# Softmax reciprocals for two heads at once, and inverse norms by logarithm and exponential, in a hybrid decoder layer

## The chip, the cores and the metric

The kernel runs on one core of one Trainium2 chip. The metric is device time of one launch in microseconds (us); lower is better. Before the change the median of three runs is 1438.42 us (1437.84 to 1440.45).

The core's engines are named as the profile names them: PE is TensorE (matmuls; PEld is its weight load), DVE is VectorE, ACT is ScalarE, POOL is GpSimd, SP issues the transfers. Each engine takes its instructions in the order in which they were built; an instruction waits until what it needs from the other engines is done, and what is queued behind it on the same engine waits too.

## What is computed

One decoder layer over 1024 tokens of width 1024, in fp32. Two places of it are touched by the change (R stands for the four heads of a group):

```python
def rms_norm(x, g):
    y = x * lax.rsqrt(jnp.mean(x * x, axis=-1, keepdims=True) + RMS_EPS)
    return y * g

# attention of one block of 128 queries: three branches, each with its own softmax and gate
p_sel = masked_softmax(ss, causal)            # selected blocks: with 16 of 16 blocks, all keys up to the query
p_win = masked_softmax(sw, window of 512)     # sliding window
o = g[..., 0:1] * o_cmp + g[..., 1:2] * o_sel + g[..., 2:3] * o_win

x = x + mix @ w_out                           # mix: NSA heads and HGRN heads side by side
h = rms_norm(x, norm_ffn)                     # the FFN's input
gate, up = split(h @ w_gate_up)
x = x + (silu(gate) * up) @ w_down
```

## The kernel before

The layer runs in stages on the one core: input projection and HGRN heads, keys and values, attention together with the output projection, gate and up products (Winograd's form), and the down product. The change lies in the attention stage and in its end, where the first products of the feed-forward part begin.

**Attention.** Queries go in blocks of 128 tokens (`qb` 0 to 7). A unit is a block, a group of four heads (`g`) and a branch (`b`: 0 selected, 1 window); there are 32 units. The loop over units first issues `score` of a unit and then `values` of the unit before it. The framework's scheduler then orders the instructions of each engine by itself, so that both mix; nothing in the source fixes that order.

- `score` (lines 892 to 928) goes over four heads. PE makes the scores in PSUM (lines 915 to 918), DVE takes the negated row maximum `nm` (line 923), ACT the exponential into `pbig` with the row sum in `den` (line 924), DVE the reciprocal of `den` (line 925), and POOL multiplies the weights by reciprocal and gate (line 926). For `qb` of 4 and more the scores take one of two double banks, `ps_s`, which comes free when the exponential has read it.
- `values` (lines 930 to 943) goes over blocks of keys. PE transposes the weights of four heads into `ps_t` (line 937, two banks), ACT copies them into the high part of `ph` (line 939), DVE makes the low part (line 940), and PE multiplies both with the values (lines 941 and 942).

**Output projection and norm.** When a block of queries is finished, two output tiles (`nsa_out`, lines 807 to 824) follow in the gaps: twelve matmuls each (lines 114 to 116), added to the residual `x1` on DVE (line 590). After the second one `norm_stats` (lines 251 to 256) squares the token tile on ACT with the row sum in `n_ss` (line 254) and calls `rsqrt` (lines 118 to 127). That is twelve instructions on one column, all on DVE: three to start (lines 121 to 123) and three rounds of three (lines 125 to 127). Seven tiles are then scaled by ACT (line 821) and by the gain on POOL (line 822); the last, tile 7, is done by one DVE instruction (line 819).

**Into the feed-forward part.** `operand` (lines 796 to 804) transposes half tiles on PE and splits them on ACT (line 803) and DVE (line 804). Tile 7's norm falls into this stretch, so that its small DVE instructions stand between such splits.

The few lines that matter most:

```python
V.reciprocal(den, den)
G.tensor_scalar(pp, pp, den, gates[:, qb, h * 3 + 1 + b:h * 3 + 2 + b], op0=OP.mult, op1=OP.mult)
...
for _ in range(3):
    V.tensor_tensor(t, y, y, op=OP.mult)
    V.scalar_tensor_tensor(t, t, -0.5, v, op0=OP.mult, op1=OP.mult)
    V.scalar_tensor_tensor(y, t, 1.5, y, op0=OP.add, op1=OP.mult)
```

## Time and profile before

| | us |
|---|---|
| median of three runs | 1438.42 (1437.84 to 1440.45) |
| span of the profiled execution, first to last instruction | 1436.3 |
| runs' median less that span | 2.1 |
| PE busy | 1371.1 (95%) |
| DVE busy | 1110.9 (77%) |
| ACT busy | 622.9 (43%) |
| POOL busy | 506.4 (35%) |

The profile is of one execution; it gives its span, and its time outside the span isn't given apart, so the difference of 2.1 us between the runs' median and the span stands for what lies around it. Attention lies between about 415 and 765 us of the span, and the gate and up products follow. PE's granted clock is 0.987 of full speed over the span and 0.99 to 1.00 in the stretches that matter here. A busy PE isn't PE at its peak, since ends of matmuls are modelled.

### The profile page before, as it was taken

What the parts mean: (1) busy time and instruction counts of PE and PEld (TensorE: products, weight loads), DVE (VectorE), ACT (ScalarE), POOL (GpSimd) and SP (SyncE); (2) the same over time, 40 slices, a digit from 0 to 9 for tenths busy, and PEclk for the clock granted to TensorE, in tenths of its full rate; (3) what the DMA queues carried; (4) which work ended last, traced back from release to release, by engine and by line L of the source; (5) the groups of instructions that cost most, each with busy time, mean ns of one, the idle gap of its engine ahead of it and who ended that gap; (6) DMA issues with size and microseconds to landing.
All of it is one profiled execution on the core that took longest, in us unless ns stands there. A gap on an engine that the chain in (4) does not pass through costs nothing.

```text
span 1436.3 us, 20189 instructions
## 1 busy us (share of the span) xinstructions
PE 1371.1 (95%) x7224; PEld 1134.7 (79%) x7224; DVE 1110.9 (77%) x1948; ACT 622.9 (43%) x1211; POOL 506.4 (35%) x412
## 2 busy tenths in 40 slices
PE   8699999999999999999998999999999999987998
PEld 6578888999977777787776888888888888865887
DVE  8985889725787888889877877777777765899796
ACT  5652333323346666566655333333333323423442
POOL 7610111102034442443427423332233310379573
PEclk9899999999999999999999999999999999988999
DMA  8541110120130001000003322222222228742252
GB/s 278 192 117 45 30 30 16 41 72 27 45 133 1 1 1 59 30 16 30 16 30 89 103 88 89 80 73 82 89 75 88 88 89 313 275 151 96 81 161 95
DMA packets 103923, 122.63 MB, mean 85 GB/s; under 512 B 5872, under 2 KB 65424, under 8 KB 103824
## 3 DMA queue, kind: packets, MB, share of 16 engines
q1 hardware_dynamic: 103824, 121.35, 26.1%
q8 instruction: 57, 0.93, 0.3%
q14 instruction: 42, 0.34, 0.1%
HBM read 101.41 MB, written 19.92 MB: 84 GB/s over the span
## 4 chain that ended last, share of the span: by engine, by line
PE 74%; DVE 17%; issue 3%; ACT 2%; POOL 2%; DMA 1%; SPq 0%; ACTq 0%; POOLq 0%; DVEq 0%
PE bank L115 8%; PE bank L116 7%; PE a L114 7%; PE bank L114 7%; PE a L115 7%; PE a L116 7%; DVE wop L108 4%; PE ps_t L114 4%; PE ps_t L115 4%; PE ps_t L116 4%; PE ps_t L937 3%; PE a L941 2%; PE a L942 2%; PE ps_t L469 1%; PE ps_s L915 1%
## 5 line engine op out<-in xcount | busy, mean ns | idle before, releaser
L107 ACT ACTIVATE wop<-rpage 128x512 fp32r<-128x512 f32 x180 | 112.2, 627 | 172.2 <-PE bank L116 70.8
L926 POOL TENSOR_SCALAR pbig<-pbig,den,gates 128x640 f32<-128x640 f32 (+7 forms) x128 | 103.7, 815 | 165.3 <-DVE den L925 146.3
L108 DVE TENSOR_TENSOR wop<-rpage,wop 128x512 fp32r<-128x512 f32 x180 | 146.6, 818 | 16.9 <-ACT wop L107 14.9
L940 DVE TENSOR_TENSOR ph<-ps_t,ph 128x512 fp32r<-128x512 f32 x126 | 84.3, 683 | 17.8 <-ACT ph L939 17.0
L939 ACT ACTIVATE ph<-ps_t 128x512 fp32r<-128x512 f32 x126 | 72.7, 595 | 48.9 <-PE ps_t L937 40.0
L1088 POOL TENSOR_TENSOR tmp<-tmp,rpage 128x512 f32<-128x512 f32 x21 | 35.2, 1676 | 131.4 <-DVE wop L108 131.4
L937 PE MATMUL ps_t<-ident,pbig 128*128 128x128 f32 x504 | 78.2, 274 | 2.1 <-POOL pbig L926 2.1
L115 PE MATMUL bank<-wop 128*128 128x512 f32 x175 | 70.8, 405 | 9.4 <-DVE wop L108 9.4
L475 POOL TENSOR_TENSOR kp<-kp,fp 128x256 f32<-128x256 f32 x28 | 20.3, 725 | 162.2 <-PE bank L452 110.7
L108 DVE TENSOR_TENSOR wop<-tmp,wop 128x512 fp32r<-128x512 f32 x42 | 40.1, 956 | 38.7 <-ACT wop L107 37.7
L937 PEld LDWEIGHTS ps_t<-ident,pbig 128*128 128x128 f32 x504 | 60.7, 140 | 11.5 <-POOL pbig L926 3.2
L1048 POOL TENSOR_TENSOR tmp<-rpage 128x512 f32<-128x512 f32 x20 | 26.3, 1315 | 123.0 <-DMA rpage<-in_w_gate_up_dram 123.0
L114 PE MATMUL bank<-wop 128*128 128x512 f32 x175 | 69.5, 398 | 0.0
L116 PE MATMUL bank<-wop 128*128 128x512 f32 x175 | 69.4, 398 | 0.0
L114 PE MATMUL a<-whi,hT_h 128*128 128x256 f32 (+1 forms) x232 | 66.6, 287 | 0.0
L115 PE MATMUL a<-wlo,hT_h 128*128 128x256 f32 (+1 forms) x232 | 66.4, 286 | 0.0
L116 PE MATMUL a<-whi,hT_l 128*128 128x256 f32 (+1 forms) x232 | 66.2, 285 | 0.0
L924 ACT ACTIVATE pbig<-ps_s,nm 128x640 f32<-128x640 f32 (+3 forms) x64 | 55.9, 876 | 23.5 <-DVE nm L923 17.5
L923 DVE TENSOR_REDUCE nm<-ps_s 128x1 f32<-128x640 f32 (+3 forms) x64 | 58.1, 914 | 4.1 <-PE ps_s L918 2.7
L941 PE MATMUL a<-ph,kv 128*128 128x512 f32 x132 | 58.6, 444 | 1.7 <-ACT ph L939 1.0
L107 ACT ACTIVATE wop<-tmp 128x512 fp32r<-128x512 f32 x42 | 26.6, 633 | 76.8 <-POOL tmp L1088 44.1
L942 PE MATMUL a<-ph,kv 128*128 128x512 f32 x132 | 57.0, 432 | 2.8 <-DVE ph L940 2.3
(514 smaller groups left out, 4541.5 us busy)
## 6 DMA issues: line engine op xcount, KB each, us to landing
rpage<-in_w_gate_up_dram SPq DMA_DIRECT2D x86, 256.0 KB, 3.3
rpage<-in_w_down_dram SPq DMA_DIRECT2D x40, 512.0 KB, 4.3
act_d<-th SPq DMA_DIRECT2D x44, 256.0 KB, 2.1
rpage<-in_w_in_dram SPq DMA_DIRECT2D x14, 512.0 KB, 5.0
xn<-in_x_dram SPq DMA_DIRECT2D x8, 512.0 KB, 3.9
wraw<-in_w_in_dram SPq DMA_DIRECT2D x16, 256.0 KB, 3.4
wraw<-in_w_in_dram SPq DMA_DIRECT2D x8, 512.0 KB, 3.6
wraw<-in_w_out_dram SPq DMA_DIRECT2D x8, 512.0 KB, 3.2
```

What stands on the lines that cost most here:

```text
L107: A.activation(hi, src, AF.Copy)
L108: V.tensor_tensor(lo, src, hi.bitcast(F32), op=OP.subtract)
L114: PE.matmul(o, ah, bh, start=first, stop=False)
L115: PE.matmul(o, ah, bl, start=False, stop=False)
L116: PE.matmul(o, al, bh, start=False, stop=last)
L923: V.tensor_reduce(nm, sv, axis=AX.XY, op=OP.max, negate=True)
L926: G.tensor_scalar(pp, pp, den, gates[:, qb, h * 3 + 1 + b:h * 3 + 2 + b], op0=OP.mult, op1=OP.mult)
L937: PE.transpose(pt[:, r * P:(r + 1) * P], wts[r][:, c0:c0 + P], ident)
L939: A.activation(ph[:, 0], pt, AF.Copy)
L940: V.tensor_tensor(ph[:, 1], pt, ph[:, 0].bitcast(F32), op=OP.subtract)
L941: PE.matmul(o, vst[b][:, kb, g, :], ph[:, 0], start=b == 0 and kb == kb0, stop=False)
L942: PE.matmul(o, vst[b][:, kb, g, :], ph[:, 1], start=False, stop=False)
```

## The change

`score` keeps the row sums of two heads in the two columns of one tile, takes one reciprocal after every second head, and only then lets POOL scale both heads' weights. `norm_stats` no longer calls `rsqrt`: DVE makes mean square plus epsilon `v`, ACT takes its logarithm and the exponential of minus half of that, and DVE refines the result by one Newton step of three instructions. `rsqrt` stays for the other norms. Comments and docstrings were dropped too, which alters no instruction.

```diff
@@ norm_stats
         ss = small.tile([P, 1], F32, name="n_ss", tag="n_ss")
         rs = small.tile([P, 1], F32, name="n_rs", tag="n_rs", bufs=NT)
+        v = small.tile([P, 1], F32, name="n_v", tag="n_v")
+        t = small.tile([P, 1], F32, name="n_t", tag="n_t")
         A.activation(junk, src, AF.Square, accum_out=ss)
-        rsqrt(rs, ss, 1, 1.0 / D, EPS)
+        V.tensor_scalar(v, ss, 1.0 / D, EPS, op0=OP.mult, op1=OP.add)
+        A.activation(t, v, AF.Ln)
+        A.activation(rs, t, AF.Exp, scale=-0.5)
+        V.scalar_tensor_tensor(t, rs, rs, v, op0=OP.mult, op1=OP.mult)
+        V.tensor_scalar(t, t, -0.5, 1.5, op0=OP.mult, op1=OP.add)
+        V.tensor_scalar(rs, rs, t, None, op0=OP.mult)
         return rs
@@ score
             res = []
+            den = None
             for r in range(4):
...
-                den = small.tile([P, 1], F32, name="den", tag="den", bufs=4)
+                if r % 2 == 0:
+                    den = small.tile([P, 2], F32, name="den", tag="den", bufs=4)
...
-                A.activation(pp.rearrange("p (i n) -> p i n", i=sv.shape[1]), sv, AF.Exp, bias=nm, accum_out=den)
-                V.reciprocal(den, den)
-                G.tensor_scalar(pp, pp, den, gates[:, qb, h * 3 + 1 + b:h * 3 + 2 + b], op0=OP.mult, op1=OP.mult)
+                A.activation(pp.rearrange("p (i n) -> p i n", i=sv.shape[1]), sv, AF.Exp, bias=nm, accum_out=den[:, r % 2:r % 2 + 1])
                 res.append(pp)
+                if r % 2:
+                    V.reciprocal(den, den)
+                    for k in range(2):
+                        gk = (h - 1 + k) * 3 + 1 + b
+                        G.tensor_scalar(res[r - 1 + k], res[r - 1 + k], den[:, k:k + 1], gates[:, qb, gk:gk + 1],
+                                        op0=OP.mult, op1=OP.mult)
             return kb0, res
```

The scheduler orders the engines anew. SP's order is the same row for row. Lines of the changed kernel are 8 to 14 higher than the same lines before.

The first place is ACT, around the norm of token tile 0 (attention of block 5). `rpage,n_ss<-x` is the square with its row sum, `pbig,den` an exponential of scores, `ph` a part of the transposed weights, `x<-x,n_rs` the scaling. Before:

```order
L254 ACTIVATE rpage,n_ss<-x_3665 128x1024
L939 ACTIVATE ph<-ps_t 128x512
L924 ACTIVATE pbig,den<-ps_s,nm 128x768
L939 ACTIVATE ph<-ps_t 128x512
L924 ACTIVATE pbig,den<-ps_s,nm 128x768
L939 ACTIVATE ph<-ps_t 128x512
L924 ACTIVATE pbig,den<-ps_s,nm 128x768
L939 ACTIVATE ph<-ps_t 128x512
L924 ACTIVATE pbig,den<-ps_s,nm 128x768
L939 ACTIVATE ph<-ps_t 128x512 x2
L821 ACTIVATE x_3665<-x_3665,n_rs 128x1024
```

Now:

```order
L257 ACTIVATE rpage,n_ss<-x_3665 128x1024
L953 ACTIVATE ph<-ps_t 128x512
L934 ACTIVATE pbig,den<-ps_s,nm 128x768
L259 ACT_TABLE_LOAD
L259 ACTIVATE n_t<-n_v 128x1
L934 ACT_TABLE_LOAD
L934 ACTIVATE pbig,den<-ps_s,nm 128x768
L260 ACTIVATE n_rs<-n_t 128x1
L934 ACTIVATE pbig,den<-ps_s,nm 128x768
L829 ACTIVATE x_3665<-x_3665,n_rs 128x1024
L953 ACTIVATE ph<-ps_t 128x512
L934 ACTIVATE pbig,den<-ps_s,nm 128x768
```

Beside the logarithm and the exponential stand two table loads, one ahead of each; all eight norms have such a pair, so there are 16 loads more than before (where the program has one, at its start). The `ph` copies, which stood between the exponentials, now come after them.

The second place is PE in the same unit. `a<-ph,kv` are matmuls of `values`, `ps_t<-ident,pbig` transposes, `ps_s` scores, `a<-whi,rpage` and `a<-wlo,rpage` an output tile. Before:

```order
L918 MATMUL ps_s<-cmask,identb 128x128
L941 MATMUL a_5999<-ph,kv_3025 128x512
L937 MATMUL ps_t<-ident,pbig 128x128 x4
L942 MATMUL a_5999<-ph,kv_3025 128x512
L915 MATMUL ps_s<-kv_3025,q 128x384
L916 MATMUL ps_s<-kv_3025,q 128x384
```

Now:

```order
L927 MATMUL ps_s<-cmask,identb 128x128
L951 MATMUL ps_t<-ident,pbig 128x128 x4
L114 MATMUL a_6113<-whi,rpage 128x512
L115 MATMUL a_6113<-wlo,rpage 128x512
L116 MATMUL a_6113<-whi,rpage 128x512
L114 MATMUL a_6113<-whi,rpage 128x512
L115 MATMUL a_6113<-wlo,rpage 128x512
L924 MATMUL ps_s<-kv_3025,q 128x384
L925 MATMUL ps_s<-kv_3025,q 128x384
```

Matmuls of an output tile moved to where two that need `ph` stood, and those that need `ph` moved behind.

The third place is DVE at the last norm, tile 7, among the operand splits. Before:

```order
L127 SCALAR_TENSOR_TENSOR n_rs<-rs_t,n_rs 128x1
L804 TENSOR_TENSOR opB<-bank,opB 128x4x128
L125 TENSOR_TENSOR rs_t<-n_rs 128x1
L804 TENSOR_TENSOR opA<-bank,opA 128x4x128
L126 SCALAR_TENSOR_TENSOR rs_t<-rs_t,rs_v 128x1
L804 TENSOR_TENSOR opC<-bank,opC 128x4x128
L127 SCALAR_TENSOR_TENSOR n_rs<-rs_t,n_rs 128x1
L108 TENSOR_TENSOR wop<-rpage,wop 128x512
L819 SCALAR_TENSOR_TENSOR x_3665<-x_3665,n_rs,rpage 128x1024
L108 TENSOR_TENSOR wop<-epage,wop 128x512
```

Now:

```order
L258 TENSOR_SCALAR n_v<-n_ss 128x1
L812 TENSOR_TENSOR opA<-bank,opA 128x4x128
L812 TENSOR_TENSOR opB<-bank,opB 128x4x128
L261 SCALAR_TENSOR_TENSOR n_t<-n_rs,n_v 128x1
L812 TENSOR_TENSOR opB<-bank,opB 128x4x128
L262 TENSOR_SCALAR n_t<-n_t 128x1
L812 TENSOR_TENSOR opB<-bank,opB 128x4x128
L263 TENSOR_SCALAR n_rs<-n_rs,n_t 128x1
L812 TENSOR_TENSOR opB<-bank,opB 128x4x128
L827 SCALAR_TENSOR_TENSOR x_3665<-x_3665,n_rs,rpage 128x1024
L812 TENSOR_TENSOR opB<-bank,opB 128x4x128 x2
L108 TENSOR_TENSOR wop<-rpage,wop 128x512
```

The scaling of tile 7 (line 819, now 827) stands two `opB` splits, an `opA` and an `opC` split earlier than it did, and the small instructions before it are fewer.

## Rows read from the trace of the kernel before

**Rows 1.** The page's chain that ended last, by engine.

```profile
PE 74%; DVE 17%; issue 3%; ACT 2%; POOL 2%; DMA 1%; SPq 0%; ACTq 0%; POOLq 0%; DVEq 0%
```

**Rows 2.** Busy time by stretch (us): the attention's two parts and its end.

```profile
core 0: us, PE busy (x) PEld busy (x) DVE busy (x) ACT busy (x) POOL busy (x), PEclk, DMA share, GB/s
415.00:560.00 145.00, 141.39 (x865) 112.23 (x864) 116.47 (x288) 93.00 (x246) 61.75 (x84) 0.99 0.03 8
560.00:765.00 205.00, 197.08 (x1110) 153.59 (x1109) 165.43 (x355) 128.10 (x248) 84.72 (x71) 1.00 0.08 30
```

**Rows 3.** Busy time in seven stretches, each from a norm's square to its scaling.

```profile
596.02:609.13 13.11, 12.25 (x69) 9.09 (x68) 12.12 (x28) 9.42 (x17) 5.19 (x5) 1.00 0.17 61
...
sum 83.06, PE 78.16 PEld 59.70 DVE 75.00 ACT 56.84 POOL 26.45; mean PE 11.17 PEld 8.53 DVE 10.71 ACT 8.12 POOL 3.78
```

**Rows 4.** Busy time in the six stretches between those, from 609.13 to 750.20 us.

```profile
sum 77.47, PE 77.03 PEld 60.75 DVE 56.66 ACT 46.22 POOL 36.60; mean PE 12.84 PEld 10.12 DVE 9.44 ACT 7.70 POOL 6.10
```

**Rows 5.** DVE in time order, first norm: start, us, what.

```profile
595.90 1.62 DVE L603 CAST rpage<-qtok 128x512 fp32r<-128x512 f32 x1
597.56 0.69 DVE L604 TENSOR_TENSOR rpage<-qtok,rpage 128x512 fp32r<-128x512 f32 x1
...
606.43 0.84 DVE L126 SCALAR_TENSOR_TENSOR rs_t<-rs_t,rs_v 128x1 f32<-128x1 f32 x1
607.20 0.68 DVE L940 TENSOR_TENSOR ph<-ps_t,ph 128x512 fp32r<-128x512 f32 x1
```

**Rows 6.** PE in time order, first norm: the waits behind those two.

```profile
599.77 0.49 PE L942 MATMUL a<-ph,kv 128*128 128x512 f32 x1 [0.39 <-DVE rs_v L121]
...
607.93 0.50 PE L942 MATMUL a<-ph,kv 128*128 128x512 f32 x1 [0.41 <-DVE ph L940]
```

**Rows 7.** DVE groups by line, 415 to 800 us: busy, mean ns, idle before.

```profile
L925 DVE RECIPROCAL den<-den 128x1 f32<-128x1 f32 x128 | 19.6, 156 | 8.1 <-ACT pbig L924 7.0
L125 DVE TENSOR_TENSOR rs_t<-n_rs 128x1 f32<-128x1 f32 x24 | 7.0, 291 | 0.2
L127 DVE SCALAR_TENSOR_TENSOR n_rs<-rs_t,n_rs 128x1 f32<-128x1 f32 x24 | 6.8, 284 | 0.2
L126 DVE SCALAR_TENSOR_TENSOR rs_t<-rs_t,rs_v 128x1 f32<-128x1 f32 x24 | 6.5, 271 | 0.3
L884 DVE RECIPROCAL c_den<-c_den 128x8 f32<-128x8 f32 x8 | 1.5, 192 | 0.0
L122 DVE TENSOR_SCALAR rs_t<-rs_v 128x1 int32<-128x1 int32 x8 | 1.2, 147 | 0.1
```

**Rows 8.** ACT in time order, the program's start: its one table load.

```profile
0.73 1.28 ACT L433 ACT_TABLE_LOAD   x1 [0.73 <-PEq L1308]
3.00 0.21 ACT L433 ACTIVATE gains<-gains 128x8 f32<-128x8 f32 x1 [0.99 <-DVE gains L432]
```

**Rows 9.** DVE in time order, the program's start.

```profile
2.82 0.16 DVE L432 TENSOR_TENSOR gains<-par_t,gains 128x4 f32<-128x4 f32 x1
```

**Rows 10.** Busy time (us) around the last norm, columns as in Rows 2.

```profile
763.13:779.24 16.11, 10.92 (x66) 7.66 (x64) 15.32 (x27) 10.03 (x18) 12.55 (x9) 1.00 0.52 135
```

**Rows 11.** DVE in time order at the last norm.

```profile
770.05 0.85 DVE L127 SCALAR_TENSOR_TENSOR n_rs<-rs_t,n_rs 128x1 f32<-128x1 f32 x1
...
771.42 0.70 DVE L125 TENSOR_TENSOR rs_t<-n_rs 128x1 f32<-128x1 f32 x1
...
772.65 0.83 DVE L126 SCALAR_TENSOR_TENSOR rs_t<-rs_t,rs_v 128x1 f32<-128x1 f32 x1
...
774.00 0.72 DVE L127 SCALAR_TENSOR_TENSOR n_rs<-rs_t,n_rs 128x1 f32<-128x1 f32 x1
```

**Rows 12.** Waits of PE and its weight load, 415 to 560 us: total, times, longest.

```profile
PE ps_t L937 <- POOL pbig L926: 2.1, 3, 1.4
...
PEld ps_t L937 <- POOL pbig L926: 3.2, 6, 1.7
```

**Rows 13.** POOL's scaling by line: times ns min/median/max over all sizes.

```profile
L926 POOL TENSOR_SCALAR pbig<-pbig,den,gates x128: 443/872/1693, 416.1 to 734.9; 128x640 f32<-128x640 f32 x40, 128x128 f32<-128x128 f32 x16, 128x256 f32<-128x256 f32 x16, 128x384 f32<-128x384 f32 x16
```

## The prediction, made before the changed kernel was run

> **What bounds the kernel now.** I read the page's chain of waits first, then busy time by stretch, then single engines in time order. In the chain PE has 74% and DVE 17%, ACT and POOL 2% each [rows 1]: a saving on DVE can count, a few us on ACT so far cost nothing. The change lies between 415 and about 780 us. In its two long parts PE is busy 141.4 of 145 and 197.1 of 205 us [rows 2], so 3.6 and 7.9 us of idle PE are all that faster other engines could give back there by this view.
>
> Where that idle time lies is the main reading. I cut the second part at the norms of the first seven token tiles, each stretch from its square to its scaling. In those seven stretches, 83.06 us together, PE is busy 78.2 and DVE 75.0, that is 90% of the time, while ACT has 56.8 (68%) [rows 3]. In the six stretches between them PE is busy 77.03 of 77.47 us [rows 4]. So PE loses its time at the norms, where DVE is nearly full, and almost none elsewhere. The first norm shows how: a cast took 1.62 us where its sister instruction took 0.69, and one of the small norm instructions 0.84 us where such a one takes 0.15 without waiting [rows 5, 7]; soon behind each of them PE stands still for 0.39 and 0.41 us [rows 6].
>
> **What leaves DVE.** Of the twelve instructions of a norm, three take 0.15 us and nine 0.27 to 0.29 on average [rows 7]: 3 x 1.2 + 7.0 + 6.8 + 6.5 = 23.9 us for eight norms, 3.0 us each. The new norm has four: three of one input, at 0.15, and one with two tensors, at 0.27, together 0.72 us; that is 2.3 us less per norm, 18 us in all. Of the 128 reciprocals at 0.156 us [rows 7] 64 go, 10 us; two columns instead of one I cost at nothing, because eight take 0.192. In the seven norm stretches DVE then has 75.0 - 16 = 59 us of 83, even before the reciprocals are counted.
>
> **What comes to ACT.** Per norm: a table load, the logarithm, a second load, the exponential. The one load of the trace took 1.28 us and an exponential of eight columns 0.21 [rows 8], so 2 x 1.28 + 2 x 0.21 = 3.0 us in which ACT serves nobody, 24 us for eight norms. In the seven stretches ACT goes from 56.8 to 56.8 + 21 = 77.8 of 83 us, or 94%. DVE and ACT change places: what was the fullest engine beside PE gets air, and the other becomes a little fuller than DVE was, in lumps.
>
> The load's price has an upper bound as well. In the only row, 0.99 us pass from its end at 2.01 to the next activation at 3.00 [rows 8]. The DVE instruction which that activation waited for ended at 2.82 + 0.16 = 2.98 [rows 9], which explains the gap, so I take 1.28; the bounds are 1.28 and 1.28 + 0.99 = 2.27.
>
> The Trainium skill, page "ScalarE: Activation LUTs", section "What ACT_TABLE_LOAD costs", speaks against this change: a switch to another table set is a load of about 1283 ns plus a drain of about 1380 ns, 2.66 us together. The trace agrees on the load [rows 8] and shows no drain, as no switch under way was recorded; by the page's figure, and as an estimate, the sum below would be 16 x 1.38 = 22 us longer, 1466 us.
>
> **Seven norms under attention.** What does a stop of 3.0 us on ACT cost PE? Behind the loads stand the next exponential, which frees a bank for the scores of a later head, and the `ph` copies that the matmuls of `values` need. The pairing adds to this: the reciprocal of a pair on DVE waits for the second head's exponential, which at the first norm is behind both loads, and the Newton step and the next row maximum are queued behind it. The scheduler put five matmuls of an output tile in front of the score, so part is covered. The nearest rows for the rest are the two waits above: 0.93 us lost on DVE became 0.39 of PE, and 0.69 us became 0.41 [rows 5, 6], so about half. Half of 3.0 is 1.5 us per norm. Against it, PE now loses 4.9 / 7 = 0.7 us per norm to a full DVE [rows 3], most of which should return: 0.5. Net +1.0 per norm, **+7 us** for seven. Bounds: -4.9 if the loads are wholly covered and all idle time returns, +21 if all 3.0 us show and nothing returns; with 0.99 us more per load, another 14.
>
> **The last norm.** From 763 to 779 us DVE is busy 15.3 of 16.1 and PE only 10.9 [rows 10]; here DVE is the bound. Four of the small instructions took 0.85, 0.70, 0.83 and 0.72 us [rows 11], 3.1 together, and in the new order none stands there any more. ACT gets 3.0 us, on 10.0 of 16.1 us busy, but its `opB` copies wait behind the loads, and the DVE splits need them. I take half of the gain, **-1.5 us**; bounds -3.1 and +3.0.
>
> **Pairs of heads in the narrow blocks.** POOL scales both heads after the second exponential, so the weights are complete one POOL instruction later. Up to 560 us PE and its weight load wait for POOL in 9 places, 5.3 us [rows 12]; with the shortest scaling, 0.44 us [rows 13], 9 x 0.44 = 4 us is the upper bound, and the 3.6 us of idle PE in this part [rows 2] are the lower one, if fewer reciprocals on DVE let everything run sooner. I take **+0.5 us**. Beyond 560 us I count nothing, since the scaling is covered by a unit of other heads' scores and values; were that cover gone, 16 units x 0.87 us [rows 13] would be 14 us.
>
> **Sum.** +7 - 1.5 + 0.5 = +6 us on the profiled execution: 1436.3 becomes 1442.3 us of span. The median of the runs lies 2.1 us above that span, so I forecast **1444.4 us** (+0.4%).
>
> **Rivals.**
> 1. *DVE's relief wins.* If the moved output matmuls cover the loads, the norm stretches lose their 4.9 us of idle PE and the last norm its 3.1: 1438.4 - 8.0 = 1430.4 us; half of it gives 1434.4. For it: PE waits for DVE at the norms, not for ACT [rows 3, 6]. Against it: ACT at 94% has less air than DVE had, and its new work comes in stops of 3.0 us instead of small pieces between others. It decides if PE has 3 us of work per norm that needs neither `ph` nor a freed score bank; the order shows five matmuls and four transposes.
> 2. *They cancel.* ACT's fullness replaces DVE's and PE loses as much as before: 1438.4 us. For it: 94% against 90%.
> 3. *A load costs more than its row.* With the 0.99 us on each of 16 loads: 1444.4 + 16 = 1460 us. Against it: that gap has its own explanation [rows 8, 9]. For it: the load here ran on an empty engine, and those to come stand between other activations.
>
> The change could fail to do what it says only if loads were merged or scheduled away; the built order shows all 16.
>
> **Chances.** About 0.2% (2.9 us) is what a measurement of this kernel can tell from no change. My forecast, slower by 3 to 12 us, has 0.42; the dearer load, slower by more, 0.16; cancelling 0.22; the relief 0.20. So faster 0.20, same 0.22, slower 0.58. The range is 1434 to 1458 us: it leaves out the better half of rival 1 and the worse part of rival 3, under 2 in 10 together. The forecast's own range is 1441.5 to 1450.
>
> **What would show it.** In the profile of the changed kernel: 17 table loads in all, and the time from a load's end to the next activation on ACT; in the stretches around the seven norms, PE's waits named for ACT (`ph`, exponentials) where DVE stood, and ACT near 78 of 83 us; DVE down by about 28 us in the stage; PE as full as before between the norms; the scaling of tile 7 earlier. I am wrong if PE's idle time at the norms shrinks, if loads are followed by a gap near 1 us, or if PE begins to wait for POOL beyond 560 us.

## The result, and the profile after

The changed kernel takes 1461.17 us (median of 4 runs, 1460.47 to 1461.86) against 1438.69 us of the kernel before on the same chip: the ratio is 1.0156, with an interval of 1.0142 to 1.0171, **22.5 us slower**. The forecast of 1444.4 us had the sign and a good quarter of the size, and the range ended 3 us too early.

The page of the changed kernel: span, busy time and the chain that ended last.

```profile
span 1459.3 us, 20095 instructions
PE 1382.6 (95%) x7224; PEld 1142.8 (78%) x7224; DVE 1094.9 (75%) x1820; ACT 644.4 (44%) x1243; POOL 504.9 (35%) x412
PE 76%; DVE 14%; ACT 5%; issue 3%; POOL 2%; DMA 1%; SPq 0%; POOLq 0%; ACTq 0%; DVEq 0%
```

In the chain ACT has gone from 2% to 5% and DVE from 17% to 14% [rows 1]: both shares have moved the way that the prediction gave. What it did not say stands in the PE row. Before, the 7224 matmuls were busy for 1371.1 us of 1436.3; now the same 7224 matmuls are busy for 1382.6 us of 1459.3. So of the 23.0 us that the span grew, 11.5 are idle time of PE (65.2 before, 76.7 now), and the other 11.5 are matmuls that **took longer**.

The seven stretches from a norm's square to its scaling, now 64.77 us together (start and end in us, then columns as in rows 2); the first and the sixth stretch and the sum.

```profile
597.07:607.12 10.05, 8.44 (x47) 6.02 (x45) 7.15 (x12) 8.43 (x15) 2.89 (x3) 1.00 0.23 80
...
732.85:743.01 10.16, 7.60 (x42) 6.36 (x41) 6.54 (x16) 8.15 (x16) 1.20 (x2) 0.87 0.07 28
...
sum 64.77, PE 49.51 PEld 36.48 DVE 43.77 ACT 58.02 POOL 10.66; mean PE 7.07 PEld 5.21 DVE 6.25 ACT 8.29 POOL 1.52
```

PE is idle for 15.3 us in them, where it was for 4.9 [rows 3]. ACT is busy for 90% of the time and DVE for 68%; before, DVE had the 90% and ACT the 68% [rows 3]. There the two have changed places.

The sixth norm shows the mechanism. First ACT in time order (start, us, what):

```profile
735.68 1.28 ACT L259 ACT_TABLE_LOAD   x1
736.97 0.20 ACT L259 ACTIVATE n_t<-n_v 128x1 f32<-128x1 f32 x1
737.19 1.28 ACT L934 ACT_TABLE_LOAD   x1
738.49 0.79 ACT L934 ACTIVATE pbig<-ps_s,nm 128x640 f32<-128x640 f32 x1
739.18 0.19 ACT L934 ACTIVATION_READ_ACCUMULATOR pbig<-ps_s,nm 128x1 f32 x1
739.27 0.19 ACT L260 ACTIVATE n_rs<-n_t 128x1 f32<-128x1 f32 x1
```

Each load takes 1.28 us, and what follows it starts 0.01 to 0.02 us behind its end. From 735.68 to 738.49, 2.8 us, ACT does nothing for anybody else. Then PE in time order, at the same place:

```profile
736.48 0.39 PE L114 MATMUL a<-whi,rpage 128*128 128x512 f32 x1
739.43 0.38 PE L924 MATMUL ps_s<-kv,q 128*128 128x256 f32 x1 [2.56 <-ACT pbig L934]
739.65 0.39 PE L956 MATMUL a<-ph,kv 128*128 128x512 f32 x1
739.88 0.40 PE L969 MATMUL a<-ph,vc_st 128*128 128x256 f32 x2
740.11 0.40 PE L969 MATMUL a<-ph,vc_up 128*128 128x256 f32 x2
740.35 0.99 PE L808 MATMUL ps_t<-ident,x 128*128 128x128 f32 x4
...
742.23 1.05 PE L951 MATMUL ps_t<-ident,pbig 128*128 128x128 f32 x4
...
744.36 0.60 PE L951 MATMUL ps_t<-ident,pbig 128*128 128x128 f32 x4
```

The next scores need the PSUM bank that the exponential behind the second load frees, so PE stands still for 2.56 us, until that exponential has run. And then four transposes take 1.05 us at 742.23, where four others of the same line take 0.60 us two us later. The windows show what differs; the third number from the end of a row is the granted clock:

```profile
730.00:735.00 5.00, 4.99 (x34) 4.07 (x32) 3.58 (x9) 3.55 (x9) 2.37 (x2) 1.00 0.26 107
735.00:740.00 5.00, 2.44 (x13) 1.64 (x12) 2.08 (x5) 4.40 (x8) 0.00 (x0) 1.00 0.00 0
740.00:745.00 5.00, 5.00 (x26) 4.51 (x25) 3.85 (x9) 4.38 (x9) 1.91 (x1) 0.66 0.00 0
745.00:750.00 5.00, 5.00 (x31) 3.91 (x30) 2.28 (x4) 1.42 (x4) 5.00 (x6) 1.00 0.01 3
```

PE is busy for 2.44 of 5 us in one window, and in the next its granted clock is 0.66 on average; cut finer, it was 0.50 (1.2 GHz of 2.4) from 741 to 743. PE then is busy all the time, for a part of it at half speed. **This stop of ACT is paid twice**: once while PE waits, and again when it has work. Added up over slices of 1 us from 560 to 900 us, one minus the granted clock comes to 13.7 us in the changed kernel and to 0.0 in the kernel before, whose clock does not fall once in this stretch. I call this sum the *lost clock* below. Not all of the 13.7 us stands behind loads. A fall of the clock follows the loads of four of the eight norms (those at 630, 735, 760 and 782 us), 8.5 us together; at the other four it stays at 1.00. One fall, 1.7 us at 576 us, comes before the first load (601.27 us), and one, 3.4 us at 805 us, behind a wait of PE that has no load in it (see the last norm below).

Waits of PE from 560 to 785 us (total, times, longest), the three longest:

```profile
PE ps_s L924 <- ACT pbig L934: 11.2, 9, 2.6
PE a L955 <- ACT ph L953: 5.3, 6, 2.5
PE a L956 <- DVE ph L954: 1.0, 3, 0.5
```

The first two are waits for ACT, for the two things that the prediction had named, exponentials and `ph` copies. The kernel before had waits for ACT there too; its three longest, from 560 to 765 us:

```profile
PE ps_s L915 <- ACT pbig L924: 3.6, 6, 0.9
PE a L942 <- DVE ph L940: 2.3, 6, 0.6
PE a L941 <- ACT ph L939: 0.7, 1, 0.7
```

Beyond 560 us PE waits nowhere for POOL's scaling of the weights (line 940). In the narrow blocks it waits for POOL for 1.5 us and its weight load for 3.2, against 2.1 and 3.2 [rows 12].

On DVE, from the groups by line, what is left of the reciprocals and of the new norm (busy, mean ns, idle before):

```profile
L937 DVE RECIPROCAL den<-den 128x2 f32<-128x2 f32 x64 | 10.2, 159 | 17.2 <-ACT pbig L934 11.6 <-ACT n_rs L260 4.8
...
L261 DVE SCALAR_TENSOR_TENSOR n_t<-n_rs,n_v 128x1 f32<-128x1 f32 x8 | 1.7, 218 | 12.3 <-ACT n_rs L260 12.3
```

The reciprocal of two columns takes 159 ns where one column took 156 [rows 7], so the prediction's nothing for the second column holds. What is new is in the idle column: DVE stands for 12.3 us in front of the Newton step of six norms, waiting for the exponential, with the next row maximum queued behind it.

### The profile page after: what moved, and what is told of

The parts are those of the page before. It is cut to its first block, busy times and chain, and to the rows that moved or that the text cites. A ratio compares the mean times of both kernels' runs of the same rounds, so it can differ in the third digit from the quotient of the medians.

```text
span 1459.3 us, 20095 instructions
## 1 busy us (share of the span) xinstructions
PE 1382.6 (95%) x7224; PEld 1142.8 (78%) x7224; DVE 1094.9 (75%) x1820; ACT 644.4 (44%) x1243; POOL 504.9 (35%) x412
## 4 chain that ended last, share of the span: by engine, by line
PE 76%; DVE 14%; ACT 5%; issue 3%; POOL 2%; DMA 1%; SPq 0%; POOLq 0%; ACTq 0%; DVEq 0%
PE bank L115 8%; PE a L114 8%; PE bank L116 8%; PE bank L114 8%; PE a L115 8%; PE a L116 8%; PE ps_t L114 4%; PE ps_t L115 4%; PE ps_t L116 4%; DVE wop L108 4%; PE ps_t L951 3%; PE a L955 2%; PE a L956 2%; PE ps_t L477 1%; PE ps_s L924 1%
## 5 line engine op out<-in xcount | busy, mean ns | idle before, releaser
L940 POOL TENSOR_SCALAR pbig<-pbig,den,gates 128x640 f32<-128x640 f32 (+7 forms) x128 | 100.3, 794 | 157.9 <-DVE den L937 116.9
L954 DVE TENSOR_TENSOR ph<-ps_t,ph 128x512 fp32r<-128x512 f32 x126 | 84.2, 684 | 20.5 <-ACT ph L953 19.6
L955 PE MATMUL a<-ph,kv 128*128 128x512 f32 x132 | 60.3, 457 | 5.9 <-ACT ph L953 5.3
L956 PE MATMUL a<-ph,kv 128*128 128x512 f32 x132 | 59.2, 448 | 1.5 <-DVE ph L954 1.0
```

The lines of the kernel that those rows point to most:

```text
L940: G.tensor_scalar(res[r - 1 + k], res[r - 1 + k], den[:, k:k + 1], gates[:, qb, gk:gk + 1], op0=OP.mult, op1=OP.mult)
L954: V.tensor_tensor(ph[:, 1], pt, ph[:, 0].bitcast(F32), op=OP.subtract)
L955: PE.matmul(o, vst[b][:, kb, g, :], ph[:, 0], start=b == 0 and kb == kb0, stop=False)
L956: PE.matmul(o, vst[b][:, kb, g, :], ph[:, 1], start=False, stop=False)
```

## The experiments

Every kernel is compared with the kernel before on the same chip; the difference is that of the two medians. Loads counts the table loads of the program; PE busy and idle are the page's, for one profiled execution; lost clock is the sum from 560 to 900 us.

| kernel | loads | median us | against before | PE busy | PE idle | lost clock |
|---|---|---|---|---|---|---|
| before | 1 | 1438.7 | | 1371.1 | 65.2 | 0.0 |
| changed | 17 | 1461.2 | +22.5 | 1382.6 | 76.7 | 13.7 |
| pairs alone | 1 | 1444.5 | +5.3 | 1377.0 | 65.0 | 3.4 |
| new norm alone | 17 | 1460.4 | +21.2 | 1381.3 | 76.2 | 11.9 |
| changed, no switch | 1 | 1443.0 | +3.9 | 1372.2 | 66.9 | 3.4 |
| before and 16 unread loads | 17 | 1457.4 | +18.2 | 1379.1 | 75.0 | 6.8 |
| the same, 14 loads | 15 | 1456.3 | +17.7 | 1382.4 | 73.5 | 10.2 |
| the same, 32 loads | 33 | 1478.9 | +40.0 | 1386.8 | 89.7 | 20.5 |
| new norm, no switch | 1 | 1440.7 | +2.1 | 1373.0 | 65.6 | 5.1 |
| pairs, narrow blocks | 1 | 1440.4 | +1.8 | 1371.8 | 65.5 | 1.7 |
| pairs, wide blocks | 1 | 1443.4 | +4.8 | 1373.0 | 67.0 | 1.7 |
| norms in groups, new | 7 | 1460.4 | +21.6 | 1379.8 | 75.9 | 13.7 |
| norms in groups, old | 1 | 1453.8 | +15.0 | 1378.5 | 72.4 | 13.7 |
| lighter norm on DVE | 1 | 1434.8 | -4.1 | 1370.6 | 62.0 | 0.0 |
| lighter, two rounds | 1 | 1439.2 | -0.2 | 1371.9 | 65.5 | 1.7 |
| lighter and pairs | 1 | 1435.9 | -3.5 | 1372.5 | 60.6 | 1.7 |
| before, one unread DVE op | 1 | 1442.4 | +3.8 | 1374.0 | 65.4 | 0.0 |
| lighter, one unread DVE op | 1 | 1439.2 | +0.6 | 1376.3 | 63.7 | 5.1 |
| 16 unread loads, one DVE op | 17 | 1457.2 | +18.6 | 1381.1 | 74.2 | 8.5 |
| changed, one table set | 3 | 1442.9 | +4.1 | 1377.7 | 64.3 | 6.8 |

**First question: is it the loads, the pairs, or the chain through ACT?** The theory was that the table loads stop ACT and PE pays with idle time and clock. The rivals were the pairs, which hold DVE behind the second head's exponential, and the longer chain DVE, ACT, ACT, DVE. Four kernels tell them apart.

*The pairs alone*: the changed kernel with the old norm.

```diff
         A.activation(junk, src, AF.Square, accum_out=ss)
-        V.tensor_scalar(v, ss, 1.0 / D, EPS, op0=OP.mult, op1=OP.add)
-        A.activation(t, v, AF.Ln)
...
+        rsqrt(rs, ss, 1, 1.0 / D, EPS)
         return rs
```

> The reciprocals of pairs alone, with the old norm: one table load. Theory (the 16 table loads stop ACT, PE idles behind them and its granted clock falls): nothing of the loss is here; 1435 to 1441 us, the granted clock 1.00 at the norms as in the kernel before. Rival (the pairing: a pair's reciprocal and two scalings come later, and everything on DVE and POOL behind them): most of the 22.5 us is here, 1448 us or more, with PE waiting for POOL or DVE beyond 560 us.

Measured: 1444.49 us, ratio 1.0037 (1.0023 to 1.0051), no wait of PE for POOL's scaling beyond 560 us. The bulk of the loss is not here. The time lies between the two windows, 3 us above the theory's and 4 below the rival's, and PE's idle time did not grow at all: its busy time did.

*The new norm alone*: the kernel before with the change's eight new lines in `norm_stats` and one reciprocal per head.

> The new norm alone, with one reciprocal per head: 17 table loads. Theory (loads): 1455 to 1463 us, nearly all of the loss, with the granted clock falling to about 0.5 at several places between 560 and 850 us. Rival (the pairing does it, by holding DVE behind the second head's exponential and so behind the loads): without the pairing under half of the loss, 1438 to 1449 us.

Measured: 1460.36 us, ratio 1.0148 (1.0132 to 1.0164). As the theory has it, nearly the whole loss is there without a pair.

*The changed kernel without a switch of tables.*

```diff
-        A.activation(t, v, AF.Ln)
+        A.activation(t, v, AF.Exp, scale=1e-3)
```

> The changed kernel with the logarithm replaced by an exponential of the same input (scale 0.001), so that ACT's table stays: the same chain ACT, DVE, ACT, ACT, DVE, the same number of instructions, one table load instead of 17. The FFN's inverse norms are other numbers, so what is computed differs. Theory (loads): 1430 to 1440 us, no fall of the granted clock at the norms, PE's idle time in the seven norm stretches back to 5 us or less from 15.3. Rival (the longer chain across three engines, or the new order of instructions, does it without any load): 1452 us or more.

Measured: 1443.04 us, ratio 1.0025 (1.0014 to 1.0035), 18.6 us less than the changed kernel (both against the kernel before on their chip); 3 us above the theory's window and far from the rival's. The chain across the engines costs little.

*Loads that nobody needs*, in the kernel before.

```diff
+        u = small.tile([P, 1], F32, name="n_u", tag="n_u")
+        A.activation(u, ss, AF.Ln)
+        A.activation(u, u, AF.Exp, scale=-0.5)
         rsqrt(rs, ss, 1, 1.0 / D, EPS)
```

> The kernel before, with a logarithm and an exponential of the sum of squares behind each square, whose result nobody reads; the old norm stays on DVE. 17 table loads, and nothing waits for them but what stands behind them on ACT. Theory (a stopped ACT is enough): 1455 to 1466 us, the norms' DVE work not relieved on top. Rival (the loss comes from the norm's results arriving later, by the chain through ACT): 1437 to 1445 us.

Measured: 1457.36 us, ratio 1.0125 (1.0110 to 1.0141). No result waits for these loads; what stands behind them on ACT's queue does. 16 loads cost 18.2 us, or 1.1 us each, 2.3 per norm; the two short activations per norm that bring them are in this price.

**Second question: how does the loss grow, and where?**

*Loads at the first seven norms only* (the two lines under `if tt < NT - 1`, with the tile's number passed in).

> The kernel before with the unread logarithm and exponential behind the squares of token tiles 0 to 6 but not behind that of tile 7: 15 table loads. All eight cost 18.2 us. If each norm's two loads cost the same: about 7/8 of that, 1454 to 1456 us. If the last norm, where DVE is the bound and the copies for DVE's splits wait behind the loads, is dearer than the others, as the granted clock falls there too: 1446 to 1452 us.

Measured: 1456.34 us, 17.7 us above the kernel before, ratio 1.0121 (1.0105 to 1.0136). So the last norm's two loads cost about half a us, with an uncertainty of some 3 us by the two intervals: it is not the dear one, and the other seven cost 2.5 us each.

*Twice the loads.*

```diff
         A.activation(u, ss, AF.Ln)
         A.activation(u, u, AF.Exp, scale=-0.5)
+        A.activation(u, ss, AF.Ln)
+        A.activation(u, u, AF.Exp, scale=-0.5)
```

> The kernel before with twice the unread pairs behind each square: logarithm, exponential, logarithm, exponential; 33 table loads, each norm stops ACT for about 6 us instead of 3. The 16 loads took 18.2 us. If the loss grows with the time that ACT is stopped: 1475 to 1482 us, and more if the second half is exposed in full, as the matmuls in front of the next scores cover only the first part: 16 loads x 1.28 + 16 x 0.2 = 24 us more idle time, 1480 us and a larger loss of clock. If a stop costs once, however long (the granted clock falls once for each): 1458 to 1468 us.

Measured: 1478.86 us, ratio 1.0276 (1.0261 to 1.0291). The second 16 loads cost 21.8 us, a little more than the first 16. Its busy row has 15.7 us more PE than that of the kernel before, again with the same number of matmuls:

```profile
PE 1386.8 (94%) x7224; PEld 1145.1 (78%) x7224; DVE 1109.5 (75%) x1948; ACT 668.0 (45%) x1275; POOL 506.5 (34%) x412
```

and its two longest waits of PE from 560 to 800 us are again for ACT:

```profile
PE a L946 <- ACT ph L944: 14.6, 8, 5.3
PE ps_s L920 <- ACT pbig L929: 10.1, 7, 3.2
```

**Third question: what are the small parts worth?** The prediction had the pairs at +0.5 us and let DVE's relief return 0.5 us per norm.

*Pairs in the narrow blocks, and in the wide ones* (the pair's branch under `qb < NARROW`, and under `qb >= NARROW`).

> Pairs of reciprocals only in the blocks of queries 0 to 3 (up to about 560 us); blocks 4 to 7 and the norm as before. The pairs in all blocks took 5.3 us more than the kernel before, with PE idle no longer than there (65.0 against 65.2 us) and PE's busy time 5.9 us longer, so the cost is in the granted clock. If the narrow blocks carry it (weights complete one POOL instruction later, the prediction's bound of 4 us): 1442 to 1445 us. If the wide blocks do: 1438 to 1441 us.

> Pairs of reciprocals only in the blocks of queries 4 to 7, the rest as before. If the wide blocks carry the cost of the pairs, as the two falls of the granted clock at 575 and 715 us in the run with all pairs suggest: 1442 to 1446 us, with such falls again. If the narrow blocks do: 1437 to 1440 us and no fall.

Measured: 1440.43 us, ratio 1.0010 (1.0001 to 1.0018), and 1443.43 us, ratio 1.0032 (1.0020 to 1.0043). The wide blocks seem to carry it, but see below.

*The new norm without pairs and without a switch.*

> The new norm without the pairs, the logarithm replaced by an exponential of the same input (scale 0.001), so one table load; the FFN's inverse norms are other numbers. With the loads gone and the pairs gone, what is left of the change is eight small instructions less on DVE per norm and two short ones more on ACT. Theory (loads and pairs are the whole loss, the relief of DVE is worth little): 1434 to 1439 us. Rival (the chain DVE, ACT, ACT, DVE is itself a loss): 1441 us or more. If the relief of DVE counts as the prediction's first rival had it, 1430 to 1434 us.

Measured: 1440.73 us, ratio 1.0012 (1.0003 to 1.0021), between the theory's window and the rival's. PE's idle time is as before, and the granted clock falls around 771 and from 784 to 791 us, at and behind the last norm. No relief shows in the time.

*A lighter norm on DVE*: the same three start steps and three Newton rounds, each instruction with one tensor as input, beside per-row scalars, where the rounds of `rsqrt` (lines 125 to 127) read two.

```diff
-        rsqrt(rs, ss, 1, 1.0 / D, EPS)
...
+        for _ in range(3):
+            V.tensor_scalar(t, rs, rs, v, op0=OP.mult, op1=OP.mult)
+            V.tensor_scalar(t, t, -0.5, 1.5, op0=OP.mult, op1=OP.add)
+            V.tensor_scalar(rs, rs, t, None, op0=OP.mult)
```

> The norm on DVE as before, number for number the same steps, with the products written as instructions with one input and per-row scalars (about 0.15 us each) where the old ones read two inputs (0.27 to 0.29): 3.0 us of small instructions per norm become about 1.8. No load and nothing on ACT. If the relief of DVE counts: 1433 to 1437 us. If not: 1437.5 to 1440 us.

Measured: 1434.75 us, ratio 0.9972 (0.9962 to 0.9982), faster than both kernels. It looked like the relief of DVE. The traces say what was relieved. Of the 72 instructions of the old rounds from 560 to 800 us, 52 took 0.14 to 0.16 us, and the other 20 took 0.22 to 0.97 us, with POOL at work for at least 95% of each. In the lighter norm none took more than 0.27 us, though POOL was at work during 30 of the 72. The durations of a norm's small instructions fell from 3.0 to 2.3 us. Two kernels were to confirm it: two rounds instead of three, and the lighter norm with the pairs.

> The norm on DVE with instructions of one input, as in the run that took 4.1 us less than the kernel before, and two Newton rounds instead of three: nine small instructions of 0.15 us instead of twelve. About 0.45 us less per norm again, so if the first 1.2 us per norm brought 4.1 us, this brings about 1.5 us more: 1432 to 1434.5 us. If DVE was no longer in the way after the first step: 1434.5 to 1436 us.

> The pairs together with the three-round norm of one-input instructions. Alone the pairs took 5.3 us more, the norm 4.1 us less. If the pairs cost because a pair's reciprocal waits on DVE with other work queued behind it, the cost should stay when DVE has more air: 1438 to 1441.5 us. If they cost only while DVE is full at the norms: 1434 to 1437 us.

Measured: 1439.20 us, ratio 1.0004 (0.9995 to 1.0013), and 1435.85 us, ratio 0.9975 (0.9965 to 0.9985). The first contradicts: three instructions less per norm, and the whole gain is gone. The second says that the pairs cost 0.6 us here (-3.5 against -4.1), where they cost 5.3 alone. Numbers that do not add up in this way point at something that all these edits share: the scheduler builds the order of the instructions anew for each of them. So three more kernels change the order and next to nothing else, by one instruction of 144 ns per norm whose result nobody reads.

```diff
+        uu = small.tile([P, 1], F32, name="n_x", tag="n_x")
+        V.tensor_scalar(uu, ss, 1.0, 0.0, op0=OP.mult, op1=OP.add)
         return rs
```

> The kernel before with one more small DVE instruction per norm (0.15 us, one input, read by nobody). Its own work is 1.2 us on DVE, off the path. Two Newton rounds instead of three gave back all that the lighter norm had gained, so the suspicion is that any change to the norm makes the scheduler build another order, which is worth some us in either direction. If so: any value from 1433 to 1445 us, but not within 1 us of the kernel before. If the order does not matter: 1438 to 1440.5 us.

> The norm of one-input instructions in three rounds (1434.75 us) with the same unread instruction added. If the gain of 4.1 us is the relief of DVE: 1434 to 1436.5 us. If it was a lucky order: 1437 us or more.

> The kernel before with the unread logarithm and exponential per norm (1457.4 us) and the same unread DVE instruction. If the 18 us are the loads': 1453 to 1462 us, whatever the order. If a good part was the order: below 1450 us.

Measured: 1442.42 us, ratio 1.0026 (1.0015 to 1.0037); 1439.24 us, ratio 1.0004 (0.9996 to 1.0013); and 1457.21 us, ratio 1.0131 (1.0117 to 1.0145). One unread instruction per norm, 1.1 us of DVE in all, made the kernel before 3.8 us slower and the lighter norm 4.7 us slower; by the two traces of the kernel before, 466 of the 7224 places in PE's order hold another matmul. The loads still cost 18.6 us against the kernel before, and 14.8 against the kernel before with the same unread instruction. **Differences of up to about 5 us between these kernels say nothing by themselves of the part that was edited; 15 us and more do, as long as the work stays where it was.** The pairs' own cost and the relief's own worth are therefore left open: both are of the size of what a new order does. Compared like with like, the lighter norm gains both times, 4.1 us without the unread instruction and 3.2 with it (1439.24 against 1442.42); the two-round run, which gains 0.2, does not fit that.

**Fourth question: would fewer loads do?**

*Norms in groups*: the squares stay where they are, the inverse norms of tiles 0 to 3 are taken behind the fourth square, those of 4 to 6 behind the seventh, that of 7 alone, and the scalings are spread over the calls that follow; once with the new chain (7 loads), once with the old one (1 load).

```diff
+                A.activation(rpage(), x1[:, t, :], AF.Square, accum_out=ssg[:, t:t + 1])
+                if t in (3, 6, 7):
+                    c0 = {3: 0, 6: 4, 7: 7}[t]
+                    inv_norms(c0, t + 1)
+                    todo.extend(range(c0, t + 1))
```

> The new norm without the pairs, its chain taken for several token tiles at once: tiles 0 to 3 behind the square of tile 3, tiles 4 to 6 behind that of tile 6, tile 7 alone, and the scalings spread over the calls that follow. 7 table loads instead of 17. Eight norms with 16 loads took 21.2 us more than the kernel before. If the number of stops sets the loss: 3/8 of that, 1444 to 1449 us. If a norm's cost lies in its other work: 1455 us or more.

> The same grouping with the old norm on DVE: three chains of twelve small instructions instead of eight, no table load but the one at the start. Five chains of 3.0 us leave DVE. If DVE's relief at the norms is worth what it takes: 1430 to 1436 us. If it is worth nothing, as the run with the chain without loads suggests: 1437 to 1441 us. The scalings come later and tiles 4 to 6 in a lump near the end, which could cost a few us at the last norm.

Measured: 1460.44 us, ratio 1.0146 (1.0131 to 1.0161), and 1453.83 us, ratio 1.0104 (1.0091 to 1.0117). The second missed both of its windows. The first lies in its rival's window, that of a cost in the norm's other work, and the second shows why. Moving the scalings costs 15 us by itself, with no load at all, so the first run alone would have misled. Between the two, six loads at three places make 6.6 us, 1.1 each, which is the price of the other runs; but these two differ in their order as well.

*One table set for both functions.* A load written out ahead of the first norm, with the first norm's ACT work kept behind it; all else as in the changed kernel.

```diff
+                if t == 0:
+                    ld = tc.keep_in_program_order(A.add_instruction(mybir.InstLoadActFuncSet(
+                        name=nc.get_next_instruction_name(), act_func_set_id=6, ins=[], outs=[])))
+                    with tc.issue_after(ld.ins):
+                        rs2 = norm_stats(x1[:, t, :], rpage())
+                else:
+                    rs2 = norm_stats(x1[:, t, :], rpage())
```

> The changed kernel, all of it and the whole computation, with one table load written out ahead of the first norm, of the set that holds both the logarithm and the exponential; the program as built then has 3 table loads instead of 17 (the third comes with the first tanh of the feed-forward part). If the loads are the loss: near the run that had an exponential in the logarithm's place (1443 us), 1438 to 1446 us. If the earlier runs without loads were fast for another reason (other numbers in the FFN's input, a lucky order): 1450 us or more.

Measured: 1442.94 us, ratio 1.0026 (1.0017 to 1.0036). Its table loads, from ACT's groups by line, and the first norm on ACT in time order:

```profile
L441 ACT ACT_TABLE_LOAD x1 | 1.3, 1283 | 0.7 <-PEq L1328 0.7
L824 ACT ACT_TABLE_LOAD x1 | 1.3, 1283 | 0.0
L1118 ACT ACT_TABLE_LOAD x1 | 1.3, 1283 | 0.0
```

```profile
598.22 1.28 ACT L824 ACT_TABLE_LOAD   x1
599.51 1.06 ACT L257 ACTIVATE rpage<-x 128x1024 f32<-128x1024 f32 x1
...
601.45 0.19 ACT L259 ACTIVATE n_t<-n_v 128x1 f32<-128x1 f32 x1
...
602.41 0.19 ACT L260 ACTIVATE n_rs<-n_t 128x1 f32<-128x1 f32 x1
```

The logarithm and the exponential now run without a load between them. The Trainium skill, page "ScalarE: Activation LUTs", section "Table sets: the hidden batching unit", names a set that holds both functions; this run agrees with it, with 3 loads where the changed kernel has 17. The same computation is 18.4 us faster without those 14 loads (+4.1 against +22.5). That settles the cause: some 18 of the 22.5 us are the table loads. What is left, 4.1 us, is of the size of what an unread instruction can do, but it has a place as well, behind the last norm (see below). PE's idle time is 64.3 us, 12.4 less than in the changed kernel and 0.9 less than in the kernel before.

## Why the prediction was wrong, step by step

**What bounds the kernel, and who takes DVE's place: right.** PE lost its time at the norms and still does, and the waits that grew are those for ACT, in the two forms that the prediction gave. That they had been waits for DVE, as it said in its first rival, was read from the first norm alone: from 560 to 765 us PE waited 4.3 us for ACT and 2.7 for DVE in the kernel before, and from 560 to 785 us it waits 16.5 and 2.3 in the changed one. ACT is at 90% in the seven stretches, for the 94% forecast.

**What leaves DVE: right in size.** The reciprocals fell from 19.6 to 10.2 us [rows 7], and the norm's small instructions from 23.9 us to 5.8 by the groups' durations, so 27.5 of the 28 us. The page's busy time of DVE fell by 16.0 only; it counts instructions that overlap once, and the plain sum of all durations fell by 26.4.

**The price of a load: right.** 1.28 us, 16 times, and behind each of the 16 the next activation starts within 0.02 us. That refutes the third rival, which added the 0.99 us of [rows 8] to each; its time of 1460 us came out nearly right for a wrong reason. The drain of 1380 ns per switch that the Trainium skill has (page "ScalarE: Activation LUTs", section "What ACT_TABLE_LOAD costs") is in no trace here; the estimate by it, 1466 us, was too long by 5.

**"Seven norms under attention", +7 us: wrong, and the step that failed.** It was the sum of 1.5 us exposed per norm, less 0.5 returned. The first half stood: between the changed kernel and the one with a single table set PE's idle time differs by 12.4 us, that is 1.55 us for each of eight norms; against the one without a switch it differs by 9.8, or 1.2 each. That it stood is in part luck: the half came from two waits, and in one of them the loss on DVE was read too small, since the casts of that line take 0.42 us at the median and not the 0.69 of the subtraction behind it. Two things were wrong with the rest.

- *No term for TensorE's clock.* The step priced a wait of PE by its length. In the changed kernel the lost clock from 560 to 900 us is 13.7 us, in the kernel before 0.0, and the busy time of the same matmuls is 11.5 us longer. I had read a granted clock of 1.00 in [rows 2] and [rows 3] and taken it for a property of the stretch. In the changed kernel it falls to 0.50 behind the loads of four norms: behind waits of PE of 2.1, 2.6 and 2.5 us, and at the last norm behind three of 0.9 to 1.4. Behind a wait of 2.5 us at 709 us it does not fall.
- *The return of 0.5 us per norm.* No run shows it beyond what a new order does. With the new norm and no switch (+2.1 us), or with the single table set (+4.1 us), the kernel is not faster than before, though ACT has no stops then and DVE has its air. Only the lighter norm came out faster, and its gain is open by the runs with the unread instruction.

With 2.5 us per norm, as the run with 14 loads measured, the term is +17.7 us in place of +7. The changed kernel's own profile says the same: the square of the last tile, ahead of which the seven norms lie, starts 17.2 us later than before (lines at the last norm). Both lie within the bounds that the step had given, -4.9 to +21; the value chosen was too small.

**"The last norm", -1.5 us: not borne out.** Loads there cost 0.5 us (18.2 against 17.7), within the bounds of -3.1 and +3.0, but the rest did not come as forecast. The square of tile 7, before and now, and a wait of PE behind that norm, in the changed kernel and in the one with a single table set:

```profile
764.06 1.05 ACT L254 ACTIVATE rpage<-x 128x1024 f32<-128x1024 f32 x1
781.23 1.04 ACT L257 ACTIVATE rpage<-x 128x1024 f32<-128x1024 f32 x1
806.40 1.09 PE L808 MATMUL bank<-ident,d 128*128 128x128 f32 x4 [3.14 <-DVE d L1077]
789.01 1.09 PE L808 MATMUL bank<-ident,d 128*128 128x128 f32 x4 [3.14 <-DVE d L1083]
```

Of the 23.0 us of span, 17.2 are lost when this square starts, so 5.8 are lost from there on, in place of -1.5. With the single table set, where no load stands at that norm, the same part loses 4.2 us (the square starts at 765.60 us, and the span is 5.7 us longer). The wait of 3.1 us is for `d`, the difference of a tile's two halves. DVE now makes it at 805.58 us behind operand splits; before, it made it at 782.33 us ahead of them, and PE did not wait for it. The same wait stands in all five kernels that have the new norm in its old place, with loads or without, and in none of those with the old or the lighter norm in that place; the clock falls with it in these two (from 805 and 788 us). Without a switch the same part loses 2.3 us, and without the pairs as well 4.1. So 2 to 4 us of the loss go with the new norm's order and not with its loads. That the wait is their cause was not tried. The claim that none of the small instructions would stand there fell too: the new order printed above has three of them between the splits, and at the last norm they start at 786.40, 787.49 and 788.15 us, with a wait of PE of 1.4 us put down to the second.

**"Pairs of heads", +0.5 us: not settled.** Beside the new norm they add 1.3 us (22.5 against 21.2), without a switch 1.7 (3.9 against 2.1), beside the lighter one 0.6 (-3.5 against -4.1), alone 5.3. The mechanism on which the bounds rested, PE waiting for POOL, did not grow.

**The rivals.** The first, that DVE's relief wins, and the second, that the two cancel, both fail on the stops of ACT, which were not covered. The range was stretched upward for the third rival alone, up to 1458 us; that it came within 3 us of the measured time is luck, since no load had the gap of that rival.

**What is shown and what is argued.** Shown: the loads make 15 to 19 us, in five pairs of kernels with and without them: the changed kernel against no switch 18.6 and against one table set 18.4, the kernel before with unread loads and without 18.2, the same with the unread DVE instruction in both 14.8, the new norm with and without a switch 19.1; between half and seven tenths of it is idle time and the rest slower matmuls, by the profiles of these pairs (9.8 and 10.4 us with and without a switch, 12.4 and 4.9 with one table set). Argued from the rows, but not tried by itself: that PE's standing still is what lowers its clock. For it: each kernel with 14 loads or more has at least 73.5 us of idle PE and 6.8 of lost clock, and those without, as far as the norms stay where they were, at most 67.0 and 5.1. The one table set's 6.8 of lost clock at 64.3 us of idle time shows that the sum of idle time alone does not tell the lost clock. Nor does the clock fall behind every wait, as the one at 709 us shows, and the falls near 576 us come before any load.

## What to carry to other kernels

Before a function is moved to ACT, look at which table set the neighbours on its queue need: 0.2 us of logarithm brought two loads of 1.28 us, and choosing one set for both functions took 18 us off. Price a stop in front of a full PE by what stands in ACT's queue behind it, and keep a second term for the matmuls at half clock that can follow the wait; here they followed it at four of eight norms. And before a difference of a few us is put down to an edit of a scheduled kernel, add an instruction that does nothing and see what that moves.

## What was not expected of the hardware

The granted clock falls at other places in programs whose matmuls are the same. The kernel with 16 unread loads and the one with 14 differ only at the last norm, near 780 us, and PE's matmuls stand in the same order in both traces; yet from 575 to 580 us, before the first load of either (597 and 599 us), the first has a clock of 1.00 and the second 0.50 (first the kernel with 16, then that with 14; columns as in rows 2):

```profile
575.00:580.00 5.00, 4.33 (x25) 3.10 (x24) 4.87 (x9) 3.29 (x8) 2.62 (x3) 1.00 0.01 3
```

```profile
575.00:580.00 5.00, 5.00 (x19) 4.21 (x20) 3.49 (x8) 2.08 (x4) 1.95 (x2) 0.50 0.00 0
```

And the first 560 us, in which no edit of the norm runs, lost 8.5 us of clock in the profiled execution of the kernel before, 11.9 in that with the unread DVE instruction and 12.0 in that with the lighter norm. So one profile's lost clock is one execution's; the medians carry the verdicts, and the profiles only the mechanism.
